# Three feature tiles in the opening sweep, other strip reads, wider value products, a later state store and new priorities in a planned hybrid-decoder kernel

## The chip, the cores and the metric

The kernel runs on one core of one Trainium2 chip. The metric is the device time of one execution in microseconds (us). Three runs of the kernel before gave 289.45, 289.83 and 290.57 us; the median is 289.83. One more execution was profiled; all views of the trace come from that one. The engines are TensorE (PE; its weight loads are listed as PEld), VectorE (DVE), ScalarE (ACT), GpSimd (POOL) and SyncE (SP), which issues most DMAs. A difference in time of about 0.5% is what a measurement of this kernel can tell from no change.

## The reference, cut to what matters

One layer of a decoder step on 512 prompt tokens and 8 sample tokens, model width 1024, all float32. One projection of the input gives nine groups of columns. Mixer A is gated linear attention (4 heads, 64 key and 128 value features); mixer B is attention over dilated windows (8 heads of 64). Both are gated, concatenated and projected, and the residual is normalised.

```python
h = jnp.einsum('btd,de->bte', x, w_in)                  # w_in is 1024 x 3600
qa, ka, va, za, ga, qb, kb, vb, gb = jnp.split(h, split_points, axis=-1)
log_a = jax.nn.log_sigmoid(jnp.einsum('btr,rk->btk', za, w_alpha2) + b_alpha) / GATE_TEMP
o_a, s_new = gla_chunked(qa * DK_A ** -0.5, ka, va, log_a, s0, chunk)
o_a = o_a * lax.rsqrt(jnp.mean(jnp.square(o_a), -1, keepdims=True) + RMS_EPS) * gla_norm_g
o_b = prompt_dilated(qb, kb, vb, rel_bias)              # or over the cached keys for the sample tokens
mix = jnp.concatenate([o_a * silu(ga), o_b * silu(gb)], axis=-1)
y = jnp.einsum('bte,ed->btd', mix, w_out)
x_new = layer_norm(ALPHA * x + y, ln_g, ln_b)
```

Outputs are the normalised rows of the prompt and the sample, the final state of mixer A for both, and the new keys and values.

## The kernel before

**Products in three parts.** The TensorE works here on a float32 type of reduced precision. Each operand is split into a high part (a cast, on ACT) and a low part (raw minus high, on DVE); `split` does both. Each product is then three matmuls: high by high, high by low, low by high (`three`). A weight tile of 128 columns needs 8 slices of depth by 2 halves of the tokens (264 and 256 columns, the first with the 8 sample tokens) by 3 = 48 matmuls.

**A planner writes the order.** The work is written as tasks, Python generators that yield operations, waits for marks (`At`) and requests for buffers (`Need`). `Plan.run` holds an estimate of time for every engine and the DMA, and at each step issues the operation that can start earliest; among equals the one with the smaller number in `PRIO` goes first. The result is one fixed list of instructions for each engine, executed in order: an instruction that waits holds back all behind it on its engine. Any change of a cost, a priority or a task can therefore change the order everywhere. Buffers come from pools: `r` (2) for raw weights, `w` (6) for split weights, `g` (27) general ones, `sv` (4) for the sample's cache and states, `pr` (4) for attention rows, `st` (3) for strips. PSUM banks are `d` (3), `s` (3) and `t` (2).

**The opening.** `FIRST` lists slices of x (eight of 128 rows) and of the weights of ka (256 columns); `first_loads` issues them on SP, `first_splits` splits them as they land, and `dense` sweeps over the eight slices with four banks: two tiles ka0 and ka1, two halves of the tokens. Then come the gate product za (32 matmuls on raw x), and the features qa0, qa1, qb, kb, vb, gb, va and ga, one weight tile after the other, all in `dense` at priority 100. `clear` zeroes two small buffers, and ACT issues four loads into one of them, wz, at the very start.

**The middle.** In the gaps of `dense`, by priority: `gate_decay` (the decays of mixer A), `gla_levels` and `gla_level` (its scores by a tree of levels), `scores`, `softmax` and `weighted` (mixer B by pairs of heads and pairs of token tiles). `softmax` adds a strip of biases to the scores. The bias table is made once (`bias_table`), written to DRAM as 8 heads by 23 copies of a row of 640, and `strips` reads from it 128 rows, each shifted by one, as 8 groups of 16. `weighted` multiplies transposed probabilities (high `pth`, low `ptl`) with values `vhl` that hold 64 high and 64 low columns; `pth` takes all 128, `ptl` the 64 high ones. The sample tokens go through POOL and DVE (`sample_logit`, `sample_value`) and, for mixer A, through ACT and DVE (`sample_gla`), which loads, updates and stores two batches of states s.

**The end.** `gate_into` turns each ga product into a gate: three activations on ACT, a product on DVE, then its bank is free. The weights of the output projection, wo, come in eight blocks of 512 KB through the two `r` buffers; `weight_splits` splits them in that order. `out_first` does the first half of the tokens, five accumulators at a time from banks `d` and `s`, first the four slices of mixer B and then those of mixer A, which `mix_a` provides; `out_unit` does the other half. `gla_state` finishes the prompt's state after the last product and stores it from ACT. `norm(3)` normalises the last 128 rows; its rows go out in three stores, the middle one from ACT.

Every operation is recorded by one helper, line 364 of the profile, so groups are told apart by the names of their tiles.

Of the kernel before, what the change touches and what calls it, by code (L numbers as in the profile page):

```python
# [20 lines left out]
P = 128  # L21
DM = 1024
KT = DM // P
NP = 512
# [27 lines left out]
T_R = 23  # L52
# [15 lines left out]


PRIO = dict(  # L70
    wload=3, wsplit=4, decay=10, res_s=8, res=8, level=22, keys_out=2, logit=50, value=20, fills=9, bias_table=7.3, gla_levels=15.3, gla_diagonal=7.7, gla_state=24, gla_queries=25, strips=14, sample_queries=48, sample_softmax=2.5, sample_values=46, sample_gla=11, mix_sample_a=8.7, mix_sample_b=16, ln_rows=17, keys_store=17.5, gla_out=26, sample_v=12, mix_tiles=33.5, scores=31, softmax=34.2, weighted=30, mix_a=18, mix_b=19, norm3=11, norm=9)
# [9 lines left out]
class Op:  # L81
# [3 lines left out]
    def __init__(self, eng, fn, args, kw):  # L85
# [13 lines left out]
        if fn == "dma_start":  # L99
            c = 640 if eng.name == "SP" else 100  # L100
# [93 lines left out]
class Plan:  # L194
# [11 lines left out]
    def pool(self, tag, n, pool):  # L206
        self.slots[tag] = [(pool, f"{tag}{i}", {}) for i in range(n)]
# [11 lines left out]
    def free(self, *xs):  # L219
        for x in xs:  # L220
            name = x.tensor.name
            self.shares[name] = self.shares.get(name, 1) - 1
            if self.shares[name] == 0:
                last = {}
                for (_, eng), end in self.uses.pop(name, {}).items():
                    last[eng] = max(last.get(eng, 0.0), end)
                tag, (pool, t, _) = self.slot_of.pop(name)
                self.slots[tag].append((pool, t, last))

    def alloc(self, need):  # L230
        for i, tag in enumerate(need.tags):
            slots = self.slots[tag]
            if len(slots) > (need.spare if i == len(need.tags) - 1 else 0):
                s = min(slots, key=lambda s: max(s[2].values(), default=0.0))
                slots.remove(s)
                pool, t, last = s
# [132 lines left out]
def trunk(ctx: ExitStack, tc: tile.TileContext, xT, xp, xs, state, ck, cv, w_in, wab, gnorm,  # L369
# [42 lines left out]
    def split(raw, hi, lo):  # L412

        yield S.copy(hi, raw)
# [90 lines left out]
    order = [g for k, g in groups.items() if k not in ("ka0", "ka1")] + wo  # L505
# [19 lines left out]
    def clear():  # L525
# [9 lines left out]
    ka_raw = []  # L535

    def first_loads():
        za = w_in[:, OFF["za"]:OFF["za"] + 16].rearrange("(k p) n -> p k n", p=P)
        for n, a, *b in FIRST:
# [5 lines left out]
            else:  # L545
                if a % 4 == 0:
                    ka_raw.append((yield Need("r", f"raw_ka{a}", [P, 4, GW])))
                rows = w_in[a * P:b[0] * P, OFF["ka"]:OFF["ka"] + GW]
                yield D.dma_start(ka_raw[a // 4][:, a % 4:a % 4 + b[0] - a, :], rows.rearrange("(k p) n -> p k n", p=P))
            mark("first")  # L550
        yield D.dma_start(zw[:, :, :16], za)
        mark("zw")
# [8 lines left out]

    ka_hl = []

    def first_splits():
        for j, (n, a, *b) in enumerate(FIRST):
            yield At("first", j + 1)
            if n == "x":
# [6 lines left out]
                yield from split(xraw[a // 2][:, a % 2, c], xh[a][:, c], xl[a][:, c])  # L574
                mark("xs")
            else:
                if a % 4 == 0:
                    hl = []
                    for x in ("hi", "lo"):
                        hl.append((yield Need("w", f"{x}_ka{a}", [P, 4, GW], F32R)))  # L580
                    ka_hl.append(hl)
                    for i in range(2):
                        g = groups[f"ka{i}"]
                        for l, y in zip((g.hi, g.lo), hl):
                            l += [y[:, k, i * P:i * P + P] for k in range(4)]
                r = slice(a % 4, a % 4 + b[0] - a)
                yield from split(ka_raw[a // 4][:, r, :], *(y[:, r, :] for y in ka_hl[a // 4]))
                for _ in range(a, b[0]):
                    mark("kas")
                if b[0] % 4 == 0:  # L590
                    free(ka_raw[a // 4])
# [92 lines left out]
    def dense():  # L684
# [6 lines left out]
        for i in range(2):  # L691
            for u in range(2):
                pk[i, u] = yield bank("ds"[i], f"ps_ka{i}{u}")
        for k in range(KT):
            for u in range(2):
                yield At("kas", k + 1)
                yield At("xs", k + 1 + (u if k == 0 else 1))
                for i in range(2):
                    yield from three(pk[i, u][:, :TW[u]], k, halves(k, u, groups[f"ka{i}"]))
        for x in ka_hl:  # L700
            free(*x)

        pz = yield bank(("t", "s"), "ps_za")
        yield At("zw")
        yield Batch(T.matmul(pz[j * 32:j * 32 + 32, :QN[j]], zw[:, k, :], xraw[k // 2][:, k % 2, Q0[j]:Q0[j] + QN[j]],
                             start=k == 0, stop=k == KT - 1, skip_group_check=True)
                    for k in range(KT) for j in range(TT))
        free(zw, *xraw)
        add(gate_decay(pz), PRIO["decay"])
# [5 lines left out]
        for i in range(2):  # L715
            yield from feature(groups[f"qa{i}"], into("qa", qa_s, i, 0.125))
# [29 lines left out]

    def gate_decay(pz):
# [8 lines left out]
        la = yield Need("g", "la", [P, 2 * NP + 2 * NB])  # L756
# [9 lines left out]
        ls = la[:, 2 * NP:].rearrange("p (m b) -> p m b", m=2)  # L766
        parts_ = [(zv[j][:, :, :P], lv[:, :, j * P:j * P + P], lv[:, :, j * P:j * P + P]) for j in range(TT)]
        parts_.append((zv[1][:, :, P:], ls, la_s))
# [18 lines left out]
    def bias_table():  # L787
# [16 lines left out]
        yield D.dma_start(tabr, tab[:, None, :].to_broadcast([HB, T_R, T_P]))  # L804
# [97 lines left out]
    def gla_state():  # L902
# [51 lines left out]
        free(kt, B["va1"])  # L954
# [796 lines left out]
```

## Time and profile before

| what | value |
|---|---|
| median of the runs shown | 289.83 us (289.45 to 290.57) |
| the profiled execution, its own time | 290.49 us |
| its span in the trace | 288.6 us |
| TensorE busy | 276.3 us, 96% of the span |
| DVE, ACT, POOL busy | 78%, 59%, 19% |
| DMA | 51.18 MB, mean 177 GB/s |
| granted TensorE clock, mean | 0.988 |

A busy time is the sum of an engine's working time, as a share of the span. Matmuls overlap their successors, so a single matmul is listed with about 0.28 us though the next starts 0.12 us later; what counts is the step from start to start. A row of a timeline gives the start, the length, the engine, the operation with what it writes and reads, and in brackets how long the engine stood idle before it and what ended that. In the list of SP and of ACT's queue (SPq, ACTq) the length is that of the issue, not of the transfer. The chain of waits goes back from the last instruction to whatever released each step.

### The profile page before, as it was taken

What the parts mean: (1) busy time and instruction counts of PE and PEld (TensorE: products, weight loads), DVE (VectorE), ACT (ScalarE), POOL (GpSimd) and SP (SyncE); (2) the same over time, 40 slices, a digit from 0 to 9 for tenths busy, and PEclk for the clock granted to TensorE, in tenths of its full rate; (3) what the DMA queues carried; (4) which work ended last, traced back from release to release, by engine and by line L of the source; (5) the groups of instructions that cost most, each with busy time, mean ns of one, the idle gap of its engine ahead of it and who ended that gap; (6) DMA issues with size and microseconds to landing.
All of it is one profiled execution on the core that took longest, in us unless ns stands there. A gap on an engine that the chain in (4) does not pass through costs nothing.

```text
span 288.6 us, 6896 instructions
## 1 busy us (share of the span) xinstructions
PE 276.3 (96%) x2638; PEld 261.0 (90%) x2638; DVE 223.9 (78%) x549; ACT 168.9 (59%) x472; POOL 54.3 (19%) x74
## 2 busy tenths in 40 slices
PE   7999999999999999999999999999999969999990
PEld 4999999998999999898999999999999969997890
DVE  3837897999889879899899877756889594339845
ACT  5757564455559757585979875454899563212002
POOL 4000001000871337203124433620000000000000
PEclk9999999999999999999999999999999979999997
DMA  7976422226945897369999994765483779731112
GB/s 215 269 194 200 127 75 75 75 79 195 314 166 170 286 265 251 112 181 276 229 191 211 261 238 136 240 182 155 120 215 106 199 259 261 115 134 73 77 75 91
DMA packets 59079, 51.18 MB, mean 177 GB/s; under 512 B 12570, under 2 KB 50468, under 8 KB 59046
## 3 DMA queue, kind: packets, MB, share of 16 engines
q1 hardware_dynamic: 58522, 50.40, 61.5%
q8 instruction: 21, 0.34, 0.6%
q10 hardware_dynamic: 524, 0.34, 0.4%
q14 instruction: 12, 0.10, 0.1%
HBM read 45.17 MB, written 6.03 MB: 177 GB/s over the span
## 4 chain that ended last, share of the span: by engine, by line
PE 78%; DVE 10%; ACT 5%; DMA 4%; issue 1%; SPq 1%; DVEq 0%; ACTq 0%
PE ps_qb L364 8%; PE ps_gb L364 8%; PE ps_y L364 8%; PE ps_yf L364 8%; PE ps_kb L364 5%; PE ps_va_f L364 4%; PE ps_vb L364 4%; PE ps_qa L364 4%; PE ps_vb_f L364 4%; PE ps_va L364 4%; PE ps_pv L364 4%; PE ps_ka L364 4%; PE ps_pt L364 3%; PE ps_s L364 3%; DMA raw_wo__3535<-in_w_out_dram 2%; PE ps_l L364 1%
## 5 line engine op out<-in xcount | busy, mean ns | idle before, releaser
L364 POOL TENSOR_TENSOR vv<-vv,pb 128x256 f32<-128x256 f32 x32 | 25.1, 818 | 47.2 <-DMA pb<-psd_s 41.4
L364 POOL TENSOR_TENSOR past<-past,qbc 128x256 f32<-128x256 f32 x32 | 25.0, 812 | 43.3 <-DMA past<-in_ck_dram 42.5
L364 ACT ACTIVATE pr<-pr,ms 128x128 f32<-128x128 f32 (+3 forms) x51 | 27.0, 549 | 7.9 <-DVE ms L364 7.8
L364 DVE CUSTOM_DVE_ANT_0 pr<-ps_s,strip 128x128 f32<-128x128 f32 (+3 forms) x32 | 14.3, 477 | 1.0 <-DMA strip<-tabr 0.8
L364 PE MATMUL ps_pt<-cf,pr 128*128 128x128 f32 x80 | 14.0, 278 | 0.3 <-DVE pt L364 0.2
L364 ACT ACTIVATE sg<-sg 128x264 f32<-128x264 f32 (+1 forms) x32 | 13.4, 419 | 0.3
L364 PE MATMUL ps_ka<-xx,hi_ka 128*128 128x264 f32 (+1 forms) x64 | 12.7, 297 | 0.8 <-ACT xx L364 0.5
L364 PEld LDWEIGHTS ps_ka<-xx,hi_ka 128*128 128x128 f32 x64 | 10.4, 193 | 1.6 <-ACT xx L364 0.7
L364 ACT ACTIVATE d<-d 128x512 f32<-128x512 f32 x13 | 7.8, 635 | 6.7 <-DVE d L364 6.7
L364 PEld LDWEIGHTS ps_pt<-cf,pr 128*128 128x128 f32 x80 | 9.3, 140 | 1.3 <-DVE pt L364 0.4
L364 DVE TENSOR_TENSOR ptl<-ps_pt,pth 128x384 fp32r<-128x384 f32 (+1 forms) x16 | 9.7, 619 | 0.4 <-ACT pth L364 0.2
L364 DVE TENSOR_TENSOR obT<-ps_pv,pvl 64x256 f32<-64x256 f32 x16 | 6.5, 413 | 4.3 <-ACT pvl L364 4.1
L364 DVE TENSOR_REDUCE o_pv<-vv 128x4 f32<-128x1024 f32 x8 | 9.7, 1212 | 0.0
L364 DVE TENSOR_REDUCE lt<-past 128x16 f32<-128x1024 f32 x8 | 9.6, 1206 | 0.0
L364 ACT CAST pth<-ps_pt 128x384 fp32r<-128x384 f32 (+1 forms) x16 | 8.4, 530 | 1.7 <-PE ps_pt L364 1.6
L364 POOL MEMSET att<- 64x512 f32 x2 | 1.0, 520 | 44.1 <-DVE ks L364 44.1
L364 PE MATMUL ps_ka<-xx,lo_ka 128*128 128x264 f32 (+1 forms) x32 | 9.1, 283 | 0.0
L364 DVE TENSOR_TENSOR xx<-x_raw,xx 128x520 fp32r<-128x520 f32 (+2 forms) x9 | 5.8, 640 | 4.1 <-ACT xx L364 4.0
L364 ACT COPY feat_y<-ps_yf 128x256 f32<-128x256 f32 x7 | 2.6, 373 | 10.7 <-PE ps_yf L364 10.7
L364 DVE TENSOR_TENSOR d<-b 128x1024 f32<-128x1024 f32 x7 | 8.5, 1216 | 0.0
L364 PE MATMUL ps_s<-kp,qh 64*128 64x128 f32 (+3 forms) x64 | 8.3, 345 | 0.0
L364 ACT COPY pvl<-ps_pv 64x256 f32<-64x256 f32 x16 | 5.7, 368 | 4.1 <-PE ps_pv L364 3.5
(540 smaller groups left out, 1092.9 us busy)
## 6 DMA issues: line engine op xcount, KB each, us to landing
past<-in_ck_dram SPq DMA_DIRECT2D x8, 512.0 KB
vv<-in_cv_dram SPq DMA_DIRECT2D x8, 512.0 KB
pb<-psd_s SPq DMA_DIRECT2D x16, 256.0 KB
qbc<-qsd SPq DMA_DIRECT2D x8, 256.0 KB
strip<-tabr SPq DMA_DIRECT2D x8, 256.0 KB
y<-in_xp_dram SPq DMA_DIRECT2D x4, 512.0 KB
x_raw<-in_xT_dram SPq DMA_DIRECT2D x7, 260.0 KB
out_dram<-y SPq DMA_DIRECT2D x3, 512.0 KB
```

The costliest lines, as they stand in the source:

```text
L364: getattr(eng.eng, op.fn)(*op.args, **op.kw)
```

## The change

Seven edits go together.

1. The opening sweep takes three weight tiles, ka0, ka1 and qa1, from one slice of 384 columns; x and weight slices alternate. The first weight load is issued by ACT; of the first two splits, one high part moves to DVE. The sweep holds six banks; qa0 follows alone.
2. The gate product za is a task of its own, `gate_ranks`, at priority 48.3, in a bank `t`. The four loads of wz move from ACT at the start to SP behind zw. One temporary of the decays is written in place.
3. The bias table has 24 copies, with the copy as the outer index of its write; a strip is read as 16 groups of 8 rows.
4. In `weighted` all but the last `ptl` product use all 128 columns of the values, so that the low by low part is added as well.
5. The copy and store of the prompt's state wait for the mark "last", set in `norm(3)` when the inverse deviation is ready.
6. The four `pr` buffers become two of 512 and two of 384 columns, and the planner gives a request the smallest that fits.
7. Priorities: decay 10 to 48.3, gla_levels 15.3 to 7.6, logit 50 to 25.7, sample_softmax 2.5 to 8.7, sample_v 12 to 9.2. The planner's price of a DMA issue from ACT rises from 100 to 400.

```diff
-T_R = 23
+T_R = 24
+ROOMS = dict(pr=[512] * 2 + [384] * 2)
 PRIO = dict(
-    wload=3, wsplit=4, decay=10, ..., logit=50, ..., gla_levels=15.3, ..., sample_softmax=2.5, ..., sample_v=12, ...)
+    wload=3, wsplit=4, decay=48.3, ..., logit=25.7, ..., gla_levels=7.6, ..., sample_softmax=8.7, ..., sample_v=9.2, ...)
-            c = 640 if eng.name == "SP" else 100
+            c = 640 if eng.name == "SP" else 400
...
-            if len(slots) > (need.spare if i == len(need.tags) - 1 else 0):
-                s = min(slots, key=lambda s: max(s[2].values(), default=0.0))
+            n = math.prod(need.shape[1:]) if tag in ROOMS else 0
+            fits = [s for s in slots if s[3] >= n]
+            if fits and len(slots) > (need.spare if i == len(need.tags) - 1 else 0):
+                s = min(fits, key=lambda s: (s[3], max(s[2].values(), default=0.0)))
...
-    def split(raw, hi, lo):
-        yield S.copy(hi, raw)
+    def split(raw, hi, lo, eng=None, rest=()):
+        yield V.tensor_copy(hi, raw) if eng is V else S.copy(hi, raw)
+        yield from rest
         yield V.tensor_tensor(lo, raw, hi.bitcast(F32), op=ALU.subtract)
...
+    first = [groups[n] for n in ("ka0", "ka1", "qa1")]
+    FW, FO = 3 * P, OFF["qa"] + P
...
-        for j in range(4):
-            yield S.dma_start(wz[j * 32:j * 32 + 18], wab[80:98])
...
-    FIRST = (("x", 0, TS[0]), ("w", 0, 1), ("x", 0, TS[1]), ("w", 1, 2), ("x", 1), ("w", 2, 4), ("x", 2), ("x", 3),
-             ("w", 4, 6), ("x", 4), ("x", 5), ("w", 6, 8), ("x", 6), ("x", 7))
+    FIRST = (("x", 0, TS[0]), ("w", 0, slice(P, FW)), ("x", 0, TS[1]), ("w", 0, slice(0, P)), ("w", 1), ("x", 1),
+             ("w", 2), ("x", 2), ("w", 3), ("x", 3), ("w", 4), ("x", 4), ("w", 5), ("x", 5), ("w", 6), ("x", 6), ("w", 7), ("x", 7))
...
+                yield (S if a == 0 and c.start else D).dma_start(first_raw[a // 2][:, a % 2, c], w_in[a * P:(a + 1) * P, FO + c.start:FO + c.stop])
...
         yield D.dma_start(zw[:, :, :16], za)
+        for j in range(4):
+            yield D.dma_start(wz[j * 32:j * 32 + 18], wab[80:98])
...
-        for i in range(2):
+        for i in range(3):
             for u in range(2):
-                pk[i, u] = yield bank("ds"[i], f"ps_ka{i}{u}")
+                pk[i, u] = yield bank(("d", "s"), f"ps_first{i}{u}")
         for k in range(KT):
...
+            for i in ((0, 1), (2,)) if k == 0 else ((0, 1, 2),):
+                for u in range(2):
+                    yield At("firsts", k + 2 if k else 1 if 0 in i else 2)
+                    yield At("xs", k + 1 + (u if k == 0 else 1))
+                    for j in i:
+                        yield from three(pk[j, u][:, :TW[u]], k, halves(k, u, first[j]))
...
+        for u in range(2):
+            add(into("qa", qa_s, 1, 0.125)(pk[2, u], u), 2)
+        yield from feature(groups["qa0"], into("qa", qa_s, 0, 0.125))
...
+    def gate_ranks():
+        yield At("zw")
+        yield At("first", len(FIRST))
+        pz = yield bank("t", "ps_za")
+        yield Batch(T.matmul(pz[j * 32:j * 32 + 32, :QN[j]], zw[:, k, :], xraw[k // 2][:, k % 2, Q0[j]:Q0[j] + QN[j]],
+                             start=k == 0, stop=k == KT - 1, skip_group_check=True)
+                    for k in range(KT) for j in range(TT))
+        free(zw, *xraw)
+        yield from gate_decay(pz)
...
-        yield D.dma_start(tabr, tab[:, None, :].to_broadcast([HB, T_R, T_P]))
+        yield D.dma_start(tabr.rearrange("h r t -> r h t"), tab[None, :, :].to_broadcast([T_R, HB, T_P]))
...
+        yield At("last")
         yield S.copy(st[:, TT - 1].rearrange("p m v -> p (m v)"), ps[:, :256])
         free(ps)
         yield S.dma_start(st_p.rearrange("(m p) v -> p m v", p=P), st[:, TT - 1])
...
-                                                 ap=[[T_P - 16, 8], [T_P - 1, 16], [1, w]]))
+                                                 ap=[[T_P - 8, 16], [T_P - 1, 8], [1, w]]))
...
-            yield T.matmul(pv[:64, o], vk[:, :64], ptl[:, k, o], start=False, stop=k == last, skip_group_check=True)
+            if k < last:
+                yield T.matmul(pv[:, o], vk, ptl[:, k, o], start=False, stop=False, skip_group_check=True)
+            else:
+                yield T.matmul(pv[:64, o], vk[:, :64], ptl[:, k, o], start=False, stop=True, skip_group_check=True)
...
             yield S.activation(rstd, nt[:, 0:1], AF.Identity, scale=rstd)
+            mark("last")
...
+    add(gate_ranks(), PRIO["decay"])
```

More of the change, by code (lines that the diff above doesn't have):

```diff
@@ L206, in pool @@
     def pool(self, tag, n, pool):
-        self.slots[tag] = [(pool, f"{tag}{i}", {}) for i in range(n)]
+        self.slots[tag] = [(pool, f"{tag}{i}", {}, r) for i, r in zip(range(n), ROOMS.get(tag, [0] * n))]
     def add(self, gen, prio):
@@ L504, in trunk @@
     wo = [Group(w_out, g * 512, f"wo{g}_", 512) for g in range(2)]
-    order = [g for k, g in groups.items() if k not in ("ka0", "ka1")] + wo
+    first = [groups[n] for n in ("ka0", "ka1", "qa1")]
+    FW, FO = 3 * P, OFF["qa"] + P
+    order = [g for g in groups.values() if g not in first] + wo
     def weight_loads():
@@ L545, in first_loads @@
             else:
[L546 to L549, printed above, removed]
+                c = b[0] if b else slice(0, FW)
+                if a % 2 == 0 and c.stop == FW:
+                    first_raw.append((yield Need(("r", "g"), f"raw_first{a}", [P, 2, FW])))
+                yield (S if a == 0 and c.start else D).dma_start(first_raw[a // 2][:, a % 2, c], w_in[a * P:(a + 1) * P, FO + c.start:FO + c.stop])
             mark("first")
         yield D.dma_start(zw[:, :, :16], za)
+        for j in range(4):
+            yield D.dma_start(wz[j * 32:j * 32 + 18], wab[80:98])
         mark("zw")
@@ L560, in first_loads @@
         yield D.dma_start(gn, gnorm)
-    ka_hl = []
     def first_splits():
@@ L573, in first_splits @@
                         l += [y[:, 0, :], y[:, 1, :]]
-                yield from split(xraw[a // 2][:, a % 2, c], xh[a][:, c], xl[a][:, c])
+                x = split(xraw[a // 2][:, a % 2, c], xh[a][:, c], xl[a][:, c])
+                yield next(x)
+                if j == 0:
+                    rest = x
+                    continue
+                yield from x
                 mark("xs")
             else:
-                if a % 4 == 0:
+                c = b[0] if b else slice(0, FW)
+                if a % 2 == 0 and c.stop == FW:
                     hl = []
                     for x in ("hi", "lo"):
-                        hl.append((yield Need("w", f"{x}_ka{a}", [P, 4, GW], F32R)))
-                    ka_hl.append(hl)
-                    for i in range(2):
-                        g = groups[f"ka{i}"]
+                        hl.append((yield Need("w" if a < 4 else "g", f"{x}_first{a}", [P, 2, FW], F32R)))
+                    first_hl.append(hl)
+                    for i, g in enumerate(first):
+                        o = slice((i + 1) % 3 * P, (i + 1) % 3 * P + P)
                         for l, y in zip((g.hi, g.lo), hl):
[L585 to L591, printed above, removed]
+                            l += [y[:, 0, o], y[:, 1, o]]
+                yield from split(first_raw[a // 2][:, a % 2, c], *(y[:, a % 2, c] for y in first_hl[a // 2]), V if j == 1 else S, rest if j == 1 else ())
+                mark("firsts")
+                if j == 1:
+                    mark("xs")
+                if a % 2 and c.stop == FW:
+                    free(first_raw[a // 2])
         add(weight_splits(), PRIO["wsplit"])
@@ L690, in dense @@
         pk = {}
-        for i in range(2):
+        for i in range(3):
             for u in range(2):
-                pk[i, u] = yield bank("ds"[i], f"ps_ka{i}{u}")
+                pk[i, u] = yield bank(("d", "s"), f"ps_first{i}{u}")
         for k in range(KT):
[L695 to L700, printed above, removed]
-            free(*x)
[L703 to L709, printed above, removed]
+            for i in ((0, 1), (2,)) if k == 0 else ((0, 1, 2),):
[4 more added lines that the diff above has]
+                        yield from three(pk[j, u][:, :TW[u]], k, halves(k, u, first[j]))
+        for x in first_hl:
+            free(*x)
         yield from make("ka", Need("g", "ka", [P, 2, NP]), 3)
```

17 lines of the change are left out of this document (7 added, 10 removed).

## The prediction, made before the changed kernel was seen

> **What bounds the kernel now.** I read the page first, then the waits of TensorE, then the stage table, and then the timelines of the places where TensorE stands still.
>
> ```profile
> span 288.6 us, 6896 instructions
> PE 276.3 (96%) x2638; PEld 261.0 (90%) x2638; DVE 223.9 (78%) x549; ACT 168.9 (59%) x472; POOL 54.3 (19%) x74
> ...
> PE ps_yf L364 <- DVE ga L364: 2.5, 1, 2.5
> PE ps_ka L364 <- ACT xx L364: 0.5, 1, 0.5
> PE ps_ka L364 <- DVE xx L364: 0.3, 1, 0.3
> ...
> 205.00:235.00 30.00, 27.03 (x244) 25.88 (x243) 24.73 (x85) 24.15 (x82) 0.00 (x0) 0.98 0.69 204
> 234.00:236.00 2.00, 2.00 (x11) 2.00 (x11) 2.00 (x5) 1.73 (x4) 0.00 (x0) 0.50 0.82 273
> ```
>
> The first two lines are the page's span and busy times; the next three say what TensorE waited for, in us, times, longest; the last two are stages, with length, then busy time of PE, PEld, DVE, ACT and POOL, granted clock, DMA share and GB/s. TensorE is the bound: it works for 276.3 of 288.6 us, so at most 12.3 us can go without removing a product, and part of that is the start and the final norm. The one long wait is 2.5 us before ps_yf. In the same place the clock falls to 0.50. So the place to understand is 226 to 238 us:
>
> ```profile
> 222.58 0.37 SPq L364 DMA_DIRECT2D raw_wo__3535<-in_w_out_dram  x1
> 223.63 0.38 SPq L364 DMA_DIRECT2D out_dram<-s  x1
> ...
> 229.48 0.62 ACT L364 CAST hi_wo__3605<-raw_wo__3535 128x512 fp32r<-128x512 f32 x1 [3.19 <-DMA raw_wo__3535<-in_w_out_dram]
> 231.66 0.37 ACT L364 ACTIVATE sg<-ps_ga 128x256 f32<-128x256 f32 x1
> ...
> 232.96 0.42 DVE L364 TENSOR_TENSOR ga<-ps_ga,sg 128x256 f32<-128x256 f32 x1
> ...
> 226.81 0.28 PE L364 MATMUL ps_ga<-xx,lo_ga__3322 128*128 128x256 f32 x1
> 226.94 0.28 PE L364 MATMUL ps_yf<-mhb,hi_wo__3346 128*128 128x264 f32 x1
> 230.61 0.29 PE L364 MATMUL ps_yf<-mlb,hi_wo__3377 128*128 128x264 f32 x1
> 233.44 0.39 PE L364 MATMUL ps_yf<-mhb,hi_wo__3346 128*128 128x264 f32 x1 [2.54 <-DVE ga L364]
> 234.02 0.42 PE L364 MATMUL ps_yf<-mhb,hi_wo__3346 128*128 128x264 f32 x1
> 234.24 0.42 PE L364 MATMUL ps_yf<-mhb,lo_wo__3347 128*128 128x264 f32 x1
> 237.25 0.29 PE L364 MATMUL ps_yf<-mlb,hi_wo__3346 128*128 128x264 f32 x1
> ```
>
> The second number is the length, the bracket the idle time before. The weights hi_wo__3346 that the product at 233.44 reads had been in use since 226.94, so it waited for something else: out_first asks for another accumulator bank, and that bank is the one in which the last ga product ended at about 227.1. To empty it, ACT must make its sigmoid and DVE its product (231.66, 232.96). ACT was idle then, but its list is in fixed order, and ahead of the sigmoid stands the cast of a weight block that landed 6.9 us after its issue (222.58 to 229.48), while a 512 KB store of the sample state, issued 1.05 us behind it, shared the DMA engines. A late load thus stopped ACT for 3.19 us and TensorE for 2.7 (230.61 + 0.12 to 233.44). Afterwards products start 0.22 us apart (234.02, 234.24) until 237.25. Between 233.44 and 237.25 there are 17 products and one transpose; at 0.12 us each that is 2.2 us, not 3.8, so the halved clock costs 1.6 more. **The whole stall is worth 4.3 us**, and it is the largest thing that a changed order could move.
>
> The skill bears on this. The Trainium skill, "TensorE: Matmul & The Clock Gate", section "Why this matters for your kernels", asks only that TensorE have no gaps over about 3 us, since one idle window brings the half clock back. Here 2.7 us was enough, so the trace disagrees with that number. By the page a gap of this size would cost 2.7 us and the sum below would lose its 1.6.
>
> **The change part by part.** Sums are made on the profiled execution, 290.49 us (span 288.6 and 1.9 around it); the median of the runs shown is 289.83, 0.66 less.
>
> *The opening.* Its rows:
>
> ```profile
> 2.60 0.43 SPq L364 DMA_DIRECT2D x_raw<-in_xT_dram  x1
> 8.21 0.68 SPq L364 DMA_DIRECT2D zw<-in_w_in_dram  x1
> 12.90 0.38 SPq L364 DMA_DIRECT2D raw_qa__200<-in_w_in_dram  x1
> ...
> 6.19 0.62 ACT L364 CAST xx<-x_raw 128x520 fp32r<-128x520 f32 x1 [0.70 <-DMA x_raw<-in_xT_dram]
> 6.85 0.70 DVE L364 TENSOR_TENSOR xx<-x_raw,xx 128x520 fp32r<-128x520 f32 x1 [0.90 <-ACT xx L364]
> 7.61 0.39 PE L364 MATMUL ps_ka<-xx,hi_ka 128*128 128x264 f32 x1 [0.34 <-DVE xx L364]
> 17.02 1.05 ACT L364 CAST hi_qa__268<-raw_qa__200 128x1024 fp32r<-128x1024 f32 x1 [2.39 <-DMA raw_qa__200<-in_w_in_dram]
> 17.98 0.38 ACT L364 ACTIVATE ka<-ps_ka 128x256 f32<-128x256 f32 x1
> ...
> 2.45 2.34 PE L364 MATMUL warm_ps<-warm 128*128 128x512 bf16 x5
> 7.61 10.32 PE ps_ka L364 x83
> 17.92 1.98 PE ps_za L364 x61
> ...
> 7.60:18.00 10.40, 10.39 (x88) 10.22 (x92) 6.70 (x12) 6.25 (x11) 0.00 (x0) 1.00 0.99 276
> ```
>
> From 7.61 on TensorE never stops: 83 products in 10.32 us, 0.124 each. Of the 96 products of ka, 13 were done by 7.61, worth 1.61 us, so the opening loses 7.61 - 1.61 = 6.0 us. No product is removed by taking qa1 along: its 48 move from a later pass into this sweep. Only the lost time can shrink. With three tiles the first slice gives 18 products in place of 12. But the second slice of x, which sets 7.61, now has 131 KB more in front of it (128 columns more in each of two weight slices, 65.5 KB each): at 276 GB/s 0.47 us. Its place in SP's queue stays the fifth (2.60), since one load went to ACT. It lands at 6.66 in place of 6.19; cast, remainder and hand-over took 1.42 us (6.19 to 7.61), so TensorE goes on at 8.08 with 19 products done: 8.08 - 19 x 0.124 = 5.72 lost. The gain is 0.28. Later slices keep up: 462 KB at 276 GB/s are 1.67 us, 18 products 2.23. The second engine in the first split and ACT's saved issues lie under the warm-up products, which run to 4.8 (2.45 + 2.34). If the bytes cost nothing, the gain is 0.75.
>
> On the other side stands the gate product za (1.98 us), now a task of its own that enters the sweep. Its load zw was issued at 8.21 behind the opening loads; these carry 0.52 MB more, 1.9 us at 276 GB/s. Where the list puts za too early by so much, TensorE waits up to 1.9 us: the opening lies between -0.75 and +1.6. I take -0.2, a switch into and out of za costing about 0.1. The weights of qa0 are covered: SP issues three more opening loads and the four wz, 7 x 0.56 (the fifth issue at 2.60, the fifteenth at 8.21) = 3.9 us later than 12.90, they land by 20.9 (4.1 after issue, 12.90 to 17.02), and are split by 23.4 (cast 1.05, remainder twice the 0.70 of half as many elements); the sweep ends at 8.08 + 125 x 0.124 + 1.98 = 25.6. The three d banks are all held by the sweep, and qa0 needs one; the first is complete 15 products (1.9 us) before the end and emptied in 0.38 (17.98). Uncovered, that would cost about 0.6.
>
> *Value products.* Rows of one head and the next:
>
> ```profile
> 147.60 0.28 PE L364 MATMUL ps_pv<-ptl,vhl 128*64 128x256 f32 x1
> 147.72 0.28 PE L364 MATMUL ps_pv<-pth,vhl 128*128 128x256 f32 x1
> 147.84 0.28 PE L364 MATMUL ps_pv<-ptl,vhl 128*64 128x256 f32 x1
> ...
> 148.07 0.33 PE L364 MATMUL ps_pv<-pth,vhl 128*128 128x256 f32 x1
> 148.25 0.28 PE L364 MATMUL ps_pv<-ptl,vhl 128*64 128x256 f32 x1
> ```
>
> 32 of the 96 products (one per head in the first half, three in the second) become 128 columns wide. The alternating ones already start 0.12 us apart, no more than the 0.124 of the sweep, whose shape doesn't change. Value: nothing, at most a few ns each. The Trainium skill, "TensorEngine Tiling (Array Packing)", section "Key Properties", says that changing the tiling mode drains TensorE. The rows show no drain inside a head; what that rule would give is the last rival.
>
> *Strips and table.* The loads take other rows of the table and 16 groups in place of 8; the table copy grows by one of 23 parts.
>
> ```profile
> L364 DVE CUSTOM_DVE_ANT_0 pr<-ps_s,strip 128x128 f32<-128x128 f32 (+3 forms) x32 | 14.3, 477 | 1.0 <-DMA strip<-tabr 0.8
> ```
>
> DVE waited 0.8 us for strips in all, and TensorE had other work then (no wait of it names them). Value 0; bounds -0.8 and, if a strip came later, +0.8.
>
> *State store later.* At the end the exponent that the last norm needs stands behind the issue of the state store:
>
> ```profile
> 282.22 0.30 ACT L364 ACTIVATE rstd<-mv,eps 128x1 f32<-128x1 f32 x1
> 282.36 0.43 ACTq L364 DMA_DIRECT2D out_dram<-st_all  x1
> 282.83 0.20 ACT L364 ACTIVATE rstd<-rstd 128x1 f32<-128x1 f32 x1 [0.32 <-ACT rstd L364]
> ```
>
> That frees 0.3 us. Behind it, copy and issue fit ahead of ACT's own store of y. Its 128 KB now travel close to the last rows of y: at 276 GB/s 0.46 us if all lies in front of them. Between -0.3 and +0.2; I take -0.2.
>
> *The rewritten list.* PRIO changes (gate decay, levels, logits, sample softmax), ROOMS fits pr tiles by size, and ACT's DMA issue is priced at 400. None costs an instruction, but the planner writes every engine's order anew, and the stall of 4.3 us is a matter of order: a cast ahead of a ready sigmoid, a store 1.05 us behind a load. Bounds: all of it goes (-4.3), or a second such wait comes. The nearest rows for a milder wait are ACT's other one for a weight block, 2.39 us, which cost TensorE nothing, and TensorE's small waits of 0.5 and 0.3. I take ACT's wait at about 1 us: TensorE's falls by 2.2, the clock stays (-1.6), and a new order brings new small waits like those of the opening, +1.0 together. Value -2.8.
>
> Sum: -0.2 - 0.2 - 2.8 = -3.2; 290.49 - 3.2 - 0.66 = **286.6**.
>
> **The rivals.**
> - *Forecast: the stall at the output projection shrinks.* 284.2 (all of 4.3 and the best opening) to 288.4. For it: nothing but order makes the stall; ACT had been free since 226.3. Against: ga, the gates, the output weights and the sample state still meet there, as the change moves none of them.
> - *The stall stays.* Store and load still collide and the cast still stands first: -0.4 alone, 290.49 - 0.4 - 0.66 = 289.4. This is also the case in which the opening and the other named parts do little, as their rows say.
> - *Slower: a second late weight block.* The next two blocks follow the same way through two raw buffers; now they land before ACT comes to them. If one lands over about 0.5 us after ACT reaches its cast (3.19 of wait made 2.7 for TensorE), each further us is lost. One more wait of 3.19 gives +2.7, the clock being down already: 289.4 + 2.7 = 292.1.
> - *The switch of mode is dear after all.* The widest step is 148.07 to 148.25, 0.06 over 0.12. The switches fall from four to two per head in the first half and from eight to two in the second, 64 in all: 64 x 0.06 = 3.8 us, so 289.4 - 3.8 = 285.6. The even steps inside a head speak against it. The skill's sentence on the drain speaks for it.
>
> **How the numbers follow.** Forecast 0.48, stall stays 0.27, second late block 0.20, dear switch 0.05. A measurement of this kernel can tell about 0.5%, 1.45 us: under 288.4 is faster, over 291.3 slower. Faster 0.48 + 0.05 = 0.53, same 0.27, slower 0.20. The likeliest case alone reaches from 284.2 to 288.4. The range goes on to 292.0, which leaves out the upper half of the third case and the edge below 284.2.
>
> **What would show it.** Opening right: TensorE continuous from about 8.1 us, za inside the sweep without a wait. Stall right: no TensorE wait over 1 us between 200 and 240 and no stage at clock 0.50 before the end; if ACT again idles over 2.5 us before a hi_wo cast, the second case holds; twice, the third. Value products right: same steps of 0.12. Tail right: 0.3 us less between the two rstd lines. A new TensorE wait over 1 us elsewhere would make the prediction wrong.

## The result, and the profile after

The changed kernel takes 288.83 us (median of 13 runs, 287.04 to 289.53); the kernel before, beside it, 290.57 (13 runs, 289.05 to 291.93). The ratio is 0.9931, with a 95% interval of 0.9903 to 0.9958: 2.0 us faster. On another chip it came out as 0.9933 (0.9903 to 0.9962). The profiled execution took 287.84 us, 2.65 less than that of before. The forecast was 286.6, in a range from 284.2 to 292.0. All ratios in this document are against the kernel before on the same chip, and executions more than 1.5% above the fastest one of their kernel are left out of them.

The page of the changed kernel, span and busy times:

```profile
span 286.1 us, 6902 instructions
PE 274.8 (96%) x2638; PEld 259.1 (91%) x2638; DVE 223.5 (78%) x546; ACT 172.1 (60%) x481; POOL 59.6 (21%) x74
```

TensorE is still the bound, with the same 2638 products. Its waits (us in total, times, longest) and two stages (the columns are those shown for before):

```profile
PE ps_va_f L368 <- DVE lo_va__2973 L368: 1.2, 2, 1.0
PE warm_ps L368 <- DVE warm L1640: 1.2, 1, 1.2
PE ps_pt L368 <- DVE va L368: 0.6, 1, 0.6
PE ps_oa L368 <- DVE oa L368: 0.6, 1, 0.6
PE ps_pt L368 <- DVE pt L368: 0.5, 1, 0.5
PE ps_first L368 <- DVE xx L368: 0.3, 1, 0.3
PE ps_yf L368 <- DVE ga L368: 0.3, 1, 0.3
```

```profile
170.00:195.00 25.00, 23.13 (x192) 22.52 (x192) 17.21 (x26) 12.42 (x30) 12.03 (x15) 1.00 0.72 193
...
205.00:235.00 30.00, 29.17 (x269) 28.00 (x268) 26.80 (x93) 26.00 (x90) 0.00 (x0) 1.00 0.69 201
```

The 2.5 us before ps_yf are now 0.3, and no stage of the output projection falls below clock 1.00. But four lines of 0.5 to 1.2 us are new or longer; the longest wait that before had between the opening and the projection was 0.4 (ps_ga). The costliest of them, in the timeline of the changed kernel; the first line is the same kind of instruction at a time when POOL was idle:

```profile
167.39 0.69 DVE L368 TENSOR_TENSOR lo_va__2748<-raw_va__2557,hi_va__2747 128x512 fp32r<-128x512 f32 x1
...
181.02 1.21 DVE L368 TENSOR_REDUCE o_pv<-vv 128x4 f32<-128x1024 f32 x1
181.45 0.62 ACT L368 CAST hi_va__2972<-raw_va__2661 128x512 fp32r<-128x512 f32 x1
182.08 3.89 POOL L368 TENSOR_TENSOR vv<-vv,pb 128x256 f32<-128x256 f32 x4 [4.35 <-DMA pb<-psd_s]
182.15 1.22 DVE L368 TENSOR_TENSOR lo_va__2973<-raw_va__2661,hi_va__2972 128x512 fp32r<-128x512 f32 x1
183.29 0.96 DVE L368 TENSOR_TENSOR mlb<-gb,mhb 128x256 fp32r<-128x256 f32 x1
184.17 1.21 DVE L368 TENSOR_TENSOR lo_va__2973<-raw_va__2661,hi_va__2972 128x512 fp32r<-128x512 f32 x1
185.43 0.39 PE L368 MATMUL ps_va_f<-xx,lo_va__2973 128*128 128x264 f32 x1 [1.02 <-DVE lo_va__2973 L368]
```

DVE's list has mlb, which nobody needs yet, between the two halves of lo_va, which TensorE needs at once; and each of the three takes about twice its time beside POOL's products (1.22 in place of 0.69; mlb 0.96, in five other places 0.41 or 0.42). The stall of before, in the changed kernel:

```profile
224.21 0.37 SPq L368 DMA_DIRECT2D raw_wo__3550<-in_w_out_dram  x1
224.68 0.41 SPq L368 DMA_DIRECT2D out_dram<-s  x1
228.84 0.62 ACT L368 CAST hi_wo__3619<-raw_wo__3550 128x512 fp32r<-128x512 f32 x1 [0.79 <-DMA raw_wo__3550<-in_w_out_dram]
230.50 0.38 ACT L368 ACTIVATE sg<-ps_ga 128x256 f32<-128x256 f32 x1
232.29 0.42 DVE L368 TENSOR_TENSOR ga<-ps_ga,sg 128x256 f32<-128x256 f32 x1
232.76 0.39 PE L368 MATMUL ps_yf<-mhb,hi_wo__3318 128*128 128x264 f32 x1 [0.27 <-DVE ga L368]
```

The pattern is the same: a cast that waits for its load, ahead of the sigmoid. The load took 4.6 us in place of 6.9, and ACT stands idle for it 0.79 us in place of 3.19. The times around it are the same: the first product of the projection starts 4.36 and 4.34 us after the issue of this load (222.58 to 226.94 before, 224.21 to 228.55 now), and from the cast to the product on DVE that frees the bank it takes 3.48 and 3.45 us. The opening and the tail:

```profile
7.68 0.39 PE L368 MATMUL ps_first<-xx,hi_first 128*128 128x264 f32 x1 [0.35 <-DVE xx L368]
17.81 2.05 PE L368 MATMUL ps_za<-x_raw,zw 128*32 128x128 f32 x64
...
280.03 0.29 ACT L368 ACTIVATE rstd<-mv,eps 128x1 f32<-128x1 f32 x1 [10.06 <-DVE mv L368]
280.35 0.20 ACT L368 ACTIVATE rstd<-rstd 128x1 f32<-128x1 f32 x1
```

To see where the time went, the span is cut at four starts of products: the first of qb, of ga and of the output projection (yf), and the last of the state (kv). The start times are those of the traces; the rows between and below the two kernels are the experiments, told further down. Each row is one execution.

| trace | to qb | qb to ga | ga to yf | yf to kv | rest | span |
|---|---|---|---|---|---|---|
| before, as predicted from | 32.46 | 160.94 | 33.53 | 54.70 | 6.97 | 288.6 |
| before_again | 33.96 | 160.68 | 33.52 | 52.23 | 6.98 | 287.4 |
| b_store_late | 32.99 | 162.28 | 33.53 | 51.30 | 6.98 | 287.1 |
| b_sigmoid_first | 32.86 | 161.73 | 33.54 | 50.58 | 6.98 | 285.7 |
| b_sig_tail | 32.88 | 161.61 | 33.52 | 51.36 | 6.66 | 286.0 |
| b_newlist | 33.55 | 162.94 | 35.38 | 50.09 | 6.99 | 288.9 |
| changed kernel | 31.75 | 163.41 | 33.39 | 50.98 | 6.53 | 286.1 |
| after_again | 32.66 | 162.77 | 33.36 | 51.58 | 6.54 | 286.9 |
| after_narrow_low | 32.24 | 163.64 | 33.40 | 50.67 | 6.54 | 286.5 |
| after_old_strips | 32.37 | 162.79 | 33.36 | 50.49 | 6.56 | 285.6 |
| a_sig | 33.35 | 163.04 | 33.39 | 50.72 | 6.60 | 287.1 |
| a_hold | 32.65 | 162.81 | 32.75 | 52.89 | 6.58 | 287.7 |
| a_hold_sig | 32.25 | 161.25 | 32.75 | 52.22 | 6.59 | 285.1 |
| a_oldlist | 32.05 | 166.99 | 31.73 | 54.34 | 6.59 | 291.7 |

From the first row to that of the changed kernel: -0.71, +2.47, -0.14, -3.72, -0.44, together -2.5. One list gives other numbers in another execution. Up to the output projection the five rows from before to b_sig_tail have the same list, and there qb to ga takes 160.68 to 162.28, median 161.61; the changed kernel, after_again, after_narrow_low, after_old_strips and a_sig share one too, with 162.77 to 163.64, median 163.04. So the middle of the changed kernel is slower by 1.4 us rather than 2.5.

### The profile page after: what moved, and what is told of

The parts are those of the page before. It is cut to its first block, busy times and chain, and to the rows that moved or that the text cites. A ratio compares the mean times of both kernels' runs of the same rounds, so it can differ in the third digit from the quotient of the medians.

```text
span 286.1 us, 6902 instructions
## 1 busy us (share of the span) xinstructions
PE 274.8 (96%) x2638; PEld 259.1 (91%) x2638; DVE 223.5 (78%) x546; ACT 172.1 (60%) x481; POOL 59.6 (21%) x74
## 4 chain that ended last, share of the span: by engine, by line
PE 67%; DVE 17%; ACT 9%; DMA 3%; issue 1%; SPq 1%; DVEq 0%; ACTq 0%
PE ps_qb L368 8%; PE ps_y L368 8%; PE ps_yf L368 7%; PE ps_gb L368 6%; PE ps_first L368 5%; PE ps_vb_f L368 4%; PE ps_vb L368 4%; PE ps_va L368 3%; PE ps_pv L368 3%; PE ps_pt L368 3%; PE ps_kb L368 2%; PE ps_qa L368 2%; ACT sg L368 2%; PE ps_s L368 2%; DMA raw_wo__3550<-in_w_out_dram 2%
## 5 line engine op out<-in xcount | busy, mean ns | idle before, releaser
L368 POOL TENSOR_TENSOR past<-past,qbc 128x256 f32<-128x256 f32 x32 | 29.0, 941 | 78.5 <-DMA past<-in_ck_dram 78.5
L368 POOL TENSOR_TENSOR vv<-vv,pb 128x256 f32<-128x256 f32 x32 | 26.3, 853 | 47.5 <-DVE gb_s L368 30.6
L368 ACT ACTIVATE pr<-pr,ms 128x128 f32<-128x128 f32 (+3 forms) x59 | 30.8, 548 | 4.5 <-DVE ms L368 4.4
L368 PE MATMUL ps_first<-xx,hi_first 128*128 128x264 f32 (+1 forms) x96 | 18.2, 289 | 0.4 <-DVE xx L368 0.3
L368 PEld LDWEIGHTS ps_first<-xx,hi_first 128*128 128x128 f32 x96 | 15.0, 190 | 1.4 <-DVE xx L368 0.5
L368 PE MATMUL ps_first<-xx,lo_first 128*128 128x264 f32 (+1 forms) x48 | 13.5, 282 | 0.0
L368 ACT ACTIVATE rstd<-mv,eps 128x1 f32<-128x1 f32 x4 | 1.1, 291 | 18.6 <-DVE mv L368 18.6
L368 PEld LDWEIGHTS ps_first<-xx,lo_first 128*128 128x128 f32 x48 | 9.0, 188 | 0.0
L368 PE MATMUL ps_pv<-pth,vhl 128*128 128x256 f32 (+1 forms) x32 | 7.7, 272 | 0.0
```

The source lines that it names most:

```text
L368: getattr(eng.eng, op.fn)(*op.args, **op.kw)
```

## The experiments

**Structure against list (a_oldlist, b_newlist).** Each keeps half of the change.

```diff
 a_oldlist: the changed kernel with
-    wload=3, ..., logit=25.7, ..., gla_levels=7.6, ..., sample_softmax=8.7, ..., sample_v=9.2, ...
+    wload=3, ..., logit=50, ..., gla_levels=15.3, ..., sample_softmax=2.5, ..., sample_v=12, ...
-            c = 640 if eng.name == "SP" else 400
+            c = 640 if eng.name == "SP" else 100
-ROOMS = dict(pr=[512] * 2 + [384] * 2)
+ROOMS = {}
 b_newlist: the kernel before with the same priorities and the price the other way round
```

> The changed kernel with the old priorities (decay alone stays at 48.3), the old price of ACT's DMA issue and pr buffers of one size: the edits of the structure without those of the list. Theory: the priorities removed the stall at the output projection (3.7 us) and brought the new waits between qb and ga (2.5 us). Then this kernel keeps the opening (-0.7) and the tail (-0.4), has the stall again with a stage at clock 0.50, has no TensorE wait over 0.6 us between 32 and 195 us, and stands at about -1.1 us against the kernel before, ratio 0.996. Rival: the stall hangs on when the last ga product meets the load, and the structure alone shifts that. Then the stall is gone here too while the middle stays free of waits, and the ratio is about 0.983.

> The kernel before with the new priorities of levels, logits, sample softmax and sample values and the new price of ACT's DMA issue, without any edit of the structure. Theory: the list alone makes the middle and the end of the changed kernel: no TensorE wait over 0.5 us at the output projection (-3.7), new waits of together 2 to 3 us between qb and ga (+2.5); ratio about 0.996. Rival: timing decides, not these priorities: the stall stays at 2 us or more while the new waits come anyway, ratio about 1.008, or both stay away, ratio 0.987.

Measured: a_oldlist 1.0197 (1.0153 to 1.0240), b_newlist 1.0068 (1.0034 to 1.0103). Both halves are slower than before; only together are they faster. Neither theory for a_oldlist holds. It has a stall of its own, before a bank of gb, in its timeline and stages:

```profile
160.00 0.28 PE L368 MATMUL ps_gb<-xx,lo_gb__2116 128*128 128x256 f32 x1
163.21 0.81 PE L368 MATMUL ps_gb<-xx,hi_gb__2302 128*128 128x264 f32 x2 [2.93 <-DVE gb L368]
```

```profile
158.95:162.36 3.41, 1.33 (x11) 1.12 (x10) 3.37 (x6) 2.47 (x6) 0.00 (x0) 1.00 0.44 147
162.36:165.77 3.41, 2.56 (x11) 2.56 (x12) 3.41 (x13) 2.46 (x7) 1.09 (x2) 0.50 1.00 267
165.77:169.18 3.41, 3.41 (x17) 3.41 (x17) 1.92 (x5) 1.70 (x4) 2.08 (x3) 0.50 1.09 251
```

A bank waited for its gate again, 2.93 us, and the half clock set in 2.08 us into the gap and lasted 6.8. But no load was late there: between the last product of that bank and its gate stand the casts of hi_va on ACT and the halves of lo_va on DVE. At the output projection TensorE waits 1.4 us for a weight block, near to the second-block case of the prediction, though ACT stood idle for that block's load only 0.41 us. In b_newlist the stall at the projection is gone (yf to kv 50.09), as the theory had it, and waits came instead: 1.5 and 1.1 us are its two longest from qb to ga, and ga to yf takes 1.85 more. That trace had the full clock; five of its twelve timed executions had a mean clock of 0.988 or less, and where the half clock came in them no trace shows. Of the list edits in the changed kernel, only the priorities of logits and of sample softmax alter the order of work on any engine when they are taken back one at a time and the program is built again; those of levels, decay and sample values, ROOMS and the price move no work alone.

**The stall itself (b_store_late, b_sigmoid_first).** The first moves the store that shared the DMA engines, the second the cast that stood ahead of the sigmoid:

```diff
+    def late_store(i, s4):
+        yield At("wo_split", 6)
+        yield sample_store(i, s4)
...
             g, i, raw = raws[j]
+            if g is wo[1] and i == 0:
+                yield At("ga1_done", 4)
```

> The kernel before, its list the same up to 223 us; the store of the second batch of sample states waits until the sixth block of output weights is split. Theory: the store, issued 1.05 us behind the load of the fourth-last weight block, slows that load. Without it the block lands about 4.6 us after its issue instead of 6.9, ACT waits about 0.9 us instead of 3.19, TensorE at most 0.5 instead of 2.5, no stage falls to clock 0.50: -3.0 to -3.9 us, ratio 0.987 to 0.990. Rival: the load is as late without the store; ACT and TensorE wait as before, ratio 1.000.

> The kernel before, its list the same up to 226 us; the split of the late weight block comes behind the gates of the last ga product, so that no sigmoid stands behind a cast that waits for a load. Theory: it is the order on ACT that carries the lateness to TensorE. The sigmoid starts by 227.5, its bank is free by 229, TensorE does not wait for ga over 0.3 us, and no stage falls to 0.50, with the load as late as before: -3.0 to -4.0 us, ratio 0.986 to 0.990. Rival: the weights of that block are due as soon as the bank, and TensorE waits for their low part about as long: within 1 us of the kernel before, ratio over 0.997.

Measured: 0.9979 (0.9946 to 1.0012) and 0.9951 (0.9928 to 0.9974). In b_store_late, and then in b_sigmoid_first:

```profile
224.45 0.37 SPq L364 DMA_DIRECT2D raw_wo__3535<-in_w_out_dram  x1
229.20 0.62 ACT L364 CAST hi_wo__3604<-raw_wo__3535 128x512 fp32r<-128x512 f32 x1 [1.22 <-DMA raw_wo__3535<-in_w_out_dram]
```

```profile
229.26 0.38 ACT L364 ACTIVATE sg<-ps_ga 128x256 f32<-128x256 f32 x1
230.44 1.12 ACT L364 CAST hi_wo__3675<-raw_wo__3535 128x512 fp32r<-128x512 f32 x2
230.57 0.42 DVE L364 TENSOR_TENSOR ga<-ps_ga,sg 128x256 f32<-128x256 f32 x1 [0.39 <-ACT sg L364]
```

The second mechanism is as told: with the sigmoid first (though only at 229.26, behind two casts of mha) TensorE does not wait for ga at all. Without the store the block lands 4.75 us after its issue, and TensorE waits 0.4; but that is one execution, and in the changed kernel the block lands as soon with the store close behind it. None of the 36 timed executions of these two kernels and of b_sig_tail, further down, has a mean clock under 0.991. But the gains are 0.6 us, which the interval does not tell from none, and 1.4 us, not 3 to 4. The size was wrong, and the next run says why.

**The kernels once more (before_again, after_again).**

> The kernel before once more, for a second trace of it. The executions of it that were timed beside the last four kernels showed a mean clock of 0.992 or more in 22 of 29; the first profiled one had 0.988, with the stage at 0.50. Theory: the stall at the output projection is always there, but in most executions it is shorter, TensorE waits under 2 us, and the half clock stays away; from the first product of the output projection to the last one of the state it takes 51 to 52.5 us, against 53.8 in the first trace and 50.1 in the changed kernel. Rival: the stall is the same in every execution, with 53.8 us and a stage at 0.50.

> The changed kernel once more, on the chip and beside the kernels of this group. Theory: its list fixes its waits: the waits of 0.3 to 1.2 us before products of ps_va_f, ps_pt and ps_oa come back at the same places, from the first product of qb to the first of ga it takes 163.4 us again within 0.5, and the ratio is 0.990 to 0.996 again. Rival: these waits are chance of one execution; the stretch is then within 0.5 of the 160.9 us of the kernel before.

The count in the first text is off: it is 24 of 29. Its 53.8 and 50.1 us are each 0.9 under the 54.70 and 50.98 of the table, which go by the starts named there. In before_again, and then in after_again:

```profile
223.81 0.37 SPq L364 DMA_DIRECT2D raw_wo__3535<-in_w_out_dram  x1
229.61 0.62 ACT L364 CAST hi_wo__3605<-raw_wo__3535 128x512 fp32r<-128x512 f32 x1 [2.26 <-DMA raw_wo__3535<-in_w_out_dram]
233.57 0.39 PE L364 MATMUL ps_yf<-mhb,hi_wo__3346 128*128 128x264 f32 x1 [1.44 <-DVE ga L364]
...
230.67:234.08 3.41, 1.97 (x17) 1.75 (x16) 3.38 (x10) 2.83 (x7) 0.00 (x0) 1.00 1.01 364
233.00:236.00 3.00, 2.43 (x18) 2.24 (x19) 3.00 (x8) 2.16 (x6) 0.00 (x0) 1.00 0.93 341
```

```profile
224.46 0.37 SPq L368 DMA_DIRECT2D raw_wo__3550<-in_w_out_dram  x1
229.69 0.62 ACT L368 CAST hi_wo__3619<-raw_wo__3550 128x512 fp32r<-128x512 f32 x1 [1.46 <-DMA raw_wo__3550<-in_w_out_dram]
233.61 0.39 PE L368 MATMUL ps_yf<-mhb,hi_wo__3318 128*128 128x264 f32 x1 [0.88 <-DVE ga L368]
```

In before_again it is the same list, the same load, landing 1.1 us sooner after its issue (5.8 us), TensorE's wait 1.44, the clock full: 52.23 from yf to kv in place of 54.70, as the theory said. In all five traces in which TensorE waits there for ga, the wait is the time from issue to landing (taken as the start of the cast) less 4.35 or 4.36 us:

| trace | issue to landing | TensorE's wait |
|---|---|---|
| before | 6.90 | 2.54 |
| before_again | 5.80 | 1.44 |
| b_store_late | 4.75 | 0.40 |
| changed kernel | 4.63 | 0.27 |
| after_again | 5.23 | 0.88 |

In after_narrow_low and after_old_strips, whose list is that of the changed kernel, it lands after 4.33 and 4.13 us and nothing waits for ga. So the new list left the order at this spot as costly as it was; what shrank the stall is that the load lands sooner.

The profiled execution from which the prediction was made belongs to the rarer kind: of 93 executions of the kernel before that were timed beside the experiments, 17 had a mean clock of 0.990 or less, as that one, with a median of 291.32 us; the other 76, all at 0.992 or more, had 288.74. Of the 25 timed executions of the changed kernel none was below 0.993. In after_again the waits at ps_va_f, ps_oa and ps_pt (pt) come back at the same size (1.2, 0.6, 0.5); qb to ga takes 162.77, 0.6 under the 163.4 told, a little more than the 0.5 allowed, and 2.1 over before_again; the wait of ps_pt for va (0.6) does not come back, and the projection's wait is 0.9.

**Value products and strips (after_narrow_low, after_old_strips).** The list of every engine is that of the changed kernel.

```diff
-            if k < last:
-                yield T.matmul(pv[:, o], vk, ptl[:, k, o], start=False, stop=False, skip_group_check=True)
-            else:
-                yield T.matmul(pv[:64, o], vk[:, :64], ptl[:, k, o], start=False, stop=True, skip_group_check=True)
+            yield T.matmul(pv[:64, o], vk[:, :64], ptl[:, k, o], start=False, stop=k == last, skip_group_check=True)
...
-    ap=[[T_P - 8, 16], [T_P - 1, 8], [1, w]]
+    ap=[[T_P - 16, 8], [T_P - 1, 16], [1, w]]
```

> The changed kernel with all products of the low probabilities 64 columns wide, as before; the list of every engine is otherwise the same. Left out with that is the low by low part. Theory: a product of 64 columns beside one of 128 costs TensorE nothing that the steps show; the time is that of the changed kernel within 0.3 us, and steps inside a head are 0.12 us as there. Rival: each of the 64 more changes of shape costs 0.06 us, 3.8 us in all, and this kernel is slower than the kernel before, ratio about 1.006.

> The changed kernel with strips read as 8 groups of 16 rows, as before; every engine's list is the same. Theory: DVE waits up to 0.8 us for strips again and no wait of TensorE names them: the time of the changed kernel within 0.3 us, ratio 0.992 to 0.995, with the strips landing later than the 3.1 us after issue of the changed kernel. Rival: DVE's wait reaches TensorE, and the kernel is 0.8 us or more above the changed one, ratio 0.996.

Measured: 0.9953 (0.9917 to 0.9989) and 0.9942 (0.9910 to 0.9975), both not to be told from the changed kernel. The first product of one head and the first of the next, in the changed kernel and in after_narrow_low:

```profile
144.26 0.38 PE L368 MATMUL ps_pv<-pth,vhl 128*128 128x256 f32 x1
...
145.20 0.33 PE L368 MATMUL ps_pv<-pth,vhl 128*128 128x256 f32 x1
```

```profile
145.11 0.38 PE L368 MATMUL ps_pv<-pth,vhl 128*128 128x256 f32 x1
...
146.03 0.33 PE L368 MATMUL ps_pv<-pth,vhl 128*128 128x256 f32 x1
```

The eight products of a head take 0.94 us with one narrow one among them and 0.92 with four. The drain at a change of mode, of which the Trainium skill speaks ("TensorEngine Tiling (Array Packing)", "Key Properties"), does not show in these steps. As to the strips, no wait of DVE names them under either reading.

**Toward a better version (b_sig_tail, a_sig, a_hold, a_hold_sig).** b_sig_tail is b_sigmoid_first with the change's fifth edit, the late state store; a_sig puts the sigmoid first in the changed kernel; a_hold takes mlb out from between the halves of lo_va; a_hold_sig does both.

```diff
+        if plan.marks["va1_"] in (2, 3):
+            yield At("va1_", 4)
         gb = B[f"gb{u}"][:, m, :]
```

> The kernel before with two edits behind 226 us: the split of the late weight block behind the gates of the last ga product, and the copy and store of the prompt's state behind the inverse deviation of the last norm. Theory: the second edit takes the 0.3 us between the last norm's two exponent lines and leaves the end of the last store as it is for the rest: 0.2 to 0.4 us under the kernel with the first edit alone (0.995), ratio 0.993 to 0.996, no worse than the changed kernel. Rival: the state's store lies in front of the last rows of y on the DMA engines and gives it back; ratio as with the first edit alone or above.

> The changed kernel, its list the same up to 227 us; only the split of the late weight block is behind the gates of the last ga product. Theory: TensorE's wait for ga at the output projection (0.3 and 0.9 us in two traces) goes, nothing else moves: 0.2 to 0.9 us under the changed kernel, ratio 0.990 to 0.993. Rival: the wait for that block's low part takes its place; ratio 0.993 to 0.996.

> The changed kernel, its list the same up to 180 us; one gate product of mixer B (gb by obT, then mhb and mlb) waits until the last block of va is split, so that DVE does not take mlb between the two halves of lo_va. Theory: this order makes TensorE's waits for lo_va (0.4 and 1.2 us in steps); they fall under 0.4 together, and with no new wait behind it the stretch from qb to ga takes 162.3 us instead of 163.4 and the ratio is about 0.9895. Rival: the planner writes the rest anew and another wait of about 1 us takes its place before the output projection; ratio 0.993 or above.

> As the kernel before this in the group, and the split of the late weight block behind the gates of the last ga product as well. Theory: it takes the 0.3 to 0.9 us also that TensorE waits for ga at the output projection; ratio 0.986 to 0.989, under every kernel so far. Rival: the block's low part is due then, and TensorE waits for it as long; ratio as without it.

Measured: b_sig_tail 0.9918 (0.9885 to 0.9952), a_sig 0.9972 (0.9942 to 1.0002), a_hold 0.9952 (0.9921 to 0.9984), a_hold_sig 0.9930 (0.9896 to 0.9964). The late store is worth what it should be: the rest falls from 6.98 to 6.66. Two local edits thus do for the old list what the whole change did; on the same chip the medians are 287.16 and 287.60, and the intervals overlap, so which of the two is faster stays open. The three variants of the changed kernel gain nothing that can be told, and all three theories fail: after_old_strips, with the list of the changed kernel, had a median of 287.61 on their chip, and they had 288.04, 287.31 and 287.39. a_hold shows how: TensorE's waits for lo_va go, but the planner writes all behind it anew, and yf to kv grows to 52.89. The profiled execution of a_hold was the slowest of its twelve (289.54 us), but that of a_hold_sig, with 286.97 under its median, shows the same growth (52.22). Two of the waits of a_hold:

```profile
PE ps_yt L368 <- ACT feat_y L368: 0.9, 1, 0.9
...
PE ps_ort L368 <- DVE o_r L368: 0.5, 1, 0.5
```

## Why the prediction was right, and where its size was off

The direction held, and so did the place: the stall at the output projection shrank, ACT's wait there being 0.79 us and, in the second trace, 1.46, where the prediction took about 1. The reason that the prediction gave is not what the runs show. It took the stall for a matter of order, a cast ahead of a ready sigmoid and a store close behind a load. Both still stand so, and the order there costs what it did; the load landed sooner, which no row of the prediction foretold. Whether the new list brought that about elsewhere stays open, so as far as the runs show it this much was luck. The measured gain is 2.0 us (of the medians 1.7), where it said 3.2. The time itself, 288.83, lies above the 284.2 to 288.4 of the case that it held likeliest, in part because the kernel before took 290.57 beside it and not the 289.83 from which it reckoned. And a wait of 1.02 before ps_va_f passes the bound of 1 us elsewhere that it had named as a sign of being wrong.

- **Rewritten list, -2.8: the term that was mis-sized.** In the pair of profiled executions the stall gave 3.72 back, near the working's 2.2 and 1.6, and the new waits, put at +1.0 from the small waits of the opening, came to +2.47 from qb to ga: together, with -0.14 from ga to yf, -1.4. Between executions at full clock it is much less: +1.4 from qb to ga (medians of five and five), -0.14, and -1.4 from yf to kv (52.23 to 50.83, the median of the four rows with the whole list), together -0.1.
- **The profiled execution was taken as the usual one.** The 1.6 us of half clock, and 1.1 of the 2.54 of waiting, were not in the second execution. The prediction took off 0.66 us for the difference between its execution and the median; yf to kv alone differs by 2.47 between the two traces. From 52.23 to the 50.58 of b_sigmoid_first it is 1.65, which fits the 1.4 measured.
- **Where the gain then comes from.** At full clock the opening (-0.5), the tail (-0.4) and the list (-0.1) give about -1; on the chip of before_again the medians at full clock are 288.80 and 287.60, 1.2 apart. The rest is in the executions with a half clock, 5 of 29 of the kernel before there and none of the changed kernel.
- **Opening, -0.2: too small.** The 131 KB ahead of the second slice of x were to cost 0.47 us; TensorE went on at 7.68 in place of 7.61. So the bound named for bytes that cost nothing, 0.75, was the better value: -0.71 in the pair. The landing of x varies by more than this: over the rows above that share an opening, to qb takes 32.46 to 33.96 (median of five 32.88) and 31.75 to 33.35 (median of seven, without a_oldlist, 32.37). za runs inside the sweep without a wait, as said, and the step into it is 0.21 us in place of 0.12, near the 0.1 that the prediction took for the switch.
- **Tail, -0.2: too small.** The gap between the two rstd lines falls from 0.61 to 0.32, as said, and nothing is given back: -0.44 in the pair, and 0.37 to 0.45 between the rows of the two kernels.
- **The range.** Its lower end does not follow from the two terms named for it: 289.83 less 4.3 and 0.75 is 284.8, not 284.2.
- **Value products and strips, 0:** right, each shown alone. The rivals of the dear switch and of the unchanged stall fall. The second late block did not come in the changed kernel; a_oldlist has a wait like it.

Not settled: why the same list lands that load 5.8 us after its issue in one execution and 6.9 in another, and why the changed list lands it after 4.1 to 5.2, all four times sooner. The store alone does not explain it: without it the load took 4.75 us, but in the changed kernel the store is issued 0.47 us behind the load in place of 1.05.

## What to carry to other kernels

Where a planner writes the order, price a change by its waits and not by its edits: the two halves of this one cost 0.7% and 2.0% alone and gave 0.7% together. A stall seen in one profiled execution is worth only what it has in the usual one, so look at the clock of every timed run, or take a second trace, before its whole length goes into a sum; the same holds for waits seen in one trace of the changed kernel. An instruction that waits for a load should not stand ahead of one that frees a PSUM bank: moving it took two lines and gave 0.5% in the old list. In the changed list, where the load lands sooner, it gave nothing.

## What the runs showed of the hardware

- TensorE's clock halved with gaps of 2.54 us (the kernel before) and 2.93 us (a_oldlist), and stayed full after 1.44 (before_again) and 1.52 (b_newlist). The Trainium skill, "TensorE: Matmul & The Clock Gate", section "Why this matters for your kernels", puts the limit at about 3 us; here both cases lie below it. In the clock records of all these traces the changes lie whole steps of 3.41 us apart. The two steps around the fall in the trace of before:

```profile
230.34:233.75 3.41, 0.87 (x7) 0.65 (x6) 3.38 (x10) 3.03 (x7) 0.00 (x0) 1.00 0.91 356
233.75:237.17 3.42, 3.42 (x18) 3.42 (x17) 3.42 (x8) 1.90 (x5) 0.00 (x0) 0.50 0.60 201
```

  In the step before a fall TensorE was idle for 2.54 us here and for 2.08 in a_oldlist; with 1.44 us (before_again) and 1.52 us (b_newlist) idle in one step the clock stayed full. In a_oldlist the next step, with 0.85 us idle, was followed by another at half clock. That the idle time is counted by these steps is argued from their spacing; no run moved a gap from one step to the next.
- The 32 remainders of 128x512 (lo_va, lo_vb, lo_wo) take 0.65 to 0.70 us on DVE when no product of POOL overlaps them, and 0.66 to 1.23 when one does. Six of them overlap POOL in the trace of before and seven in before_again; in those of the changed kernel and of after_again it is twelve. The waits for lo_va, 1.2 us of the changed kernel's 2.3 in the middle, lie beside such work. No run took POOL's work away, so that it makes these waits is argued and not shown.
